# Four dot products on VectorE move from the lowest priority to the taps' priority

## The chip, the cores and the metric

The kernel runs on one core of a Trainium2 chip. The metric is the device time of one execution in microseconds (us); the time before is the median of three runs, 2440.19 us (2438.97 to 2441.34). The engines are called as in the profile: PE is TensorE (matmuls), PEld its weight loads, DVE is VectorE, ACT is ScalarE, POOL is GpSimd, SP is SyncE, which here only issues DMAs.

## The reference

A block of two layers works on 1024 latent tokens of width 1024. Layer 0 has a recurrent mixer, layer 1 a convolution mixer, and each layer ends with a gated feed-forward part with a 3x3 convolution over a grid of 16 rows by 64 columns. The mixers and feed-forward parts are scaled by six modulation vectors per layer, which are products of `silu(c)` with a 1024x6144 matrix:

```python
mod = s_c @ ada_w[i] + ada_b[i]
sh1, sc1, g1, sh2, sc2, g2 = [t[:, None, :] for t in jnp.split(mod, 6, axis=-1)]
...
xm2 = rmsnorm(h, norm_ffn[i]) * (1.0 + sc2) + sh2
h = h + g2 * conv_ffn(xm2, ffn_w_up[i], ffn_conv_w[i], ffn_conv_b[i], ffn_w_down[i], ROWS, GRID_W)
...
def conv_ffn(xm, w_up, cw, cb, w_down, rows, width):
    u = dwconv2d(xm @ w_up, cw, cb, rows, width)
    v, g = jnp.split(u, 2, axis=-1)
    return (jax.nn.silu(g) * v) @ w_down
```

`g2` of layer 0 is the second gate of that layer. It is needed when the first output of the first feed-forward part is added to `h`, and not before.

## The kernel before

Channels lie on the 128 partitions, tokens along the free axis. Every float32 product is made of three matmuls with a high and a low part of each operand (`xmh`, `xml` for data, `whi`, `wlo` for weights): a weight block is loaded into `wraw`, ACT copies it to `whi`, POOL or DVE subtracts to get `wlo` (`split`).

**The first feed-forward part** (`ffn` with l = 0, from line 1063 on) goes through 22 pairs p. A pair is two column tiles of the up-projection, each 128 channels by 1024 tokens, 48 matmuls, into one of three PSUM tiles in rotation (`nt % 3`). In this text the column tiles are numbered from 0: tiles 0 and 1 are pair 0, tiles 2 and 3 pair 1, and so on. After a column tile `ffn_conv` runs the nine taps of the convolution from PSUM into an SBUF tile `cv`: the centre tap on ACT (`cv<-ps,vec`), the other eight on DVE (`cv<-ps,vec,cv`). So a column tile cannot begin on PE before the taps of the tile three before it are done. Then ACT makes the silu (`cv<-cv`), DVE the product (`cv<-cv,cv`), ACT and POOL the parts `zh` and `zl`.

**The down-projection** runs between the up-projection's matmuls from pair 3 on (column tile 6): `between()` puts a `unit` of 12 matmuls after each four steps of a column tile. A unit writes the fourth PSUM tile, and DVE adds the unit's result times `g2` to `h` (`h<-ps,mod,h`, the flush). There is one such PSUM tile, so a unit waits on PE for the flush of the unit before. Its weights come in quarters (`load_down`): a load of 256 KB into `raw`, split into `dnh` and `dnl`.

**The gate.** `g2` of layer 0 has eight columns (numbers 40 to 47 of `mod`). Each is the product of a loaded 128x1024 block with `sC`, summed along the free axis (`ada_dot`, line 543). Columns 40 to 43 are made on DVE by one instruction each (`raw,mod<-raw,sC`), called in `first_tiles` of pair 0 (line 1157). Columns 44 to 47 are made by POOL (product) and ACT (sum), called in pairs 1 and 2 (line 1151); then `ada_bias` (line 1153) adds the bias on DVE (`mod<-mod,vec`). All flushes read the result.

**Two `raw` buffers** in rotation serve these blocks and the quarters of the down weights: columns 40, 42, 44, the quarter 0, column 47 and quarter 2 take the one (`raw_76`), columns 41, 43, 45, 46 and quarter 1 the other (`raw_77`). A buffer is loaded again when its last reader is done.

**What sets the order.** `Order` collects the instructions of DVE, ACT, POOL and SP in a pool while PE's matmuls are written in program order, with a duration for each from a formula. It always emits the instruction that can start first; among those that could start at the same time the smaller `prio` goes first, then the older (`_best`, lines 110 to 126). On the chip each engine runs its list in that order and waits in it. The taps of column tiles have priority 0, flushes -1, and the four dots on DVE priority 3. In `ada_dot` a `prio` that isn't zero also lets the load go without the wait for `after`.

Of the kernel before, what the change touches and what calls it, by code (L numbers as in the profile page):

```python
# [280 lines left out]
class Net:  # L281
# [258 lines left out]

    def ada_dot(self, l, q, eng="dve", after=(), prio=0):

        t, b = self.load_raw(self.a["ada"][l, q], after=() if prio else after)
        col, mB = self.mod[l][:, q:q + 1], self.modB[l][q // 8]
        if eng == "dve":
            self.stt(1024, t, t, 1.0, self.sC, MULT, MULT, [b, self.sCB], [b], [mB], accum=col, after=after, prio=prio)
        else:
            self.tten(1024, t, t, self.sC, MULT, [b, self.sCB], [b], eng=eng, prio=prio)  # L550
            self.act(1024, t, t, AF.Copy, [b], [b], [mB], accum=col)
# [511 lines left out]
    def ffn(self, l, end, last=None):  # L1063
# [40 lines left out]
        def quarter(g, q):  # L1104
            quarters[g, q] = load_down(g, q * 256, 256, dn.next())
# [12 lines left out]
        def zsplit(p, a, aB):  # L1118
            zh, zl, zhB, zlB = zr.next()
            Z[p] = zh, zl, [[zhB, zlB]] * 2  # L1120
            self.act(1024, zh, a, AF.Copy, [aB], [zhB])
            self.tten(1024, zl, a, zh.bitcast(F32), SUB, [aB, zhB], [zlB], eng="pool")

        def last_gate(f, pt, a, aB, acc, accB):

            zh, zl, zhB, zlB = zr.next()
            Z[NF - 1] = zh, zl, [[Buf(after=[b]) for b in (zhB, zlB)] for _ in range(2)]
            for h in range(2):
                b, c = Buf(after=[aB, accB]), slice(h * 512, h * 512 + 512)
                (hB, lB), av, gv = Z[NF - 1][2][h], a[:, c], acc[:, c]  # L1130
                self.ffn_conv(l, f, pt, acc, b, h * 8, h * 8 + 8, -2)
                silu = self.act(512, gv, gv, AF.Silu, [b], [b])
                self.tten(512, av, av, gv, MULT, [b], [b], prio=-3)
                self.act(512, zh[:, c], av, AF.Copy, [b], [hB])
                self.tten(512, zl[:, c], av, zh[:, c].bitcast(F32), SUB, [b, hB], [lB], prio=-3)
            self.sqrt_soon([silu])

        nt = 0
        ada = [(0, q) for q in range(40, 48)] + [(1, q) for q in range(48)] if l == 0 else []
# [4 lines left out]
        for p in range(NF):  # L1144
            if p >= 3 and p % 2 == 1 and p < NF - 1:
                g = (p - 3) // 2
                todo += [(g, q, d) for q in range(4) for d in (2 * q, 2 * q + 1)]
            pts, accs = [], []
            if ada and 0 < p < 3:
                for _ in range(2):  # L1150
                    self.ada_dot(*ada.pop(0), "pool", prio=3)
                if p == 2:
                    self.ada_bias(0, 5)
            for q in ((), (0,), (1, 2))[p] if p < 3 else ():
                quarter(0, q)
            if p == 0:
                self.first_tiles((0, 1), lambda ops: [self.ada_dot(*ada.pop(0), prio=3, after=ops) for _ in range(4)] if ada else None)
                pts, nt = [0, 1], 2
            for i, f in enumerate((p, NF + p)):
                if p:  # L1160
                    self.col_tile(self.w_next(), nt % 3, between)
                    pts.append(nt % 3)
                    nt += 1
                acc, accB = cv.next()
                accs.append((acc, accB))
                if f < 2 * NF - 1:
                    self.ffn_conv(l, f, pts[i], acc, accB)
            (a, aB), (gt, gB) = accs
            if p < NF - 1:
                self.act(1024, gt, gt, AF.Silu, [gB], [gB])  # L1170
                self.tten(1024, a, a, gt, MULT, [aB, gB], [aB])
                zsplit(p, a, aB)
            else:
                last_gate(2 * NF - 1, pts[1], a, aB, gt, gB)
            for _ in range(3 if p > 2 else 0):
                if ada:
                    self.ada_dot(*ada.pop(0), "pool", prio=3)
# [279 lines left out]
```

## Time and profile before

| | |
|---|---|
| median of three runs | 2440.19 us |
| the profiled execution: time | 2438.16 us |
| the profiled execution: span, first to last instruction | 2436.4 us |
| granted TensorE clock, mean over the span | 0.979 |
| first feed-forward part | about 560 to 1313 us of the span |

Of the profile four kinds of views are used: the page of the whole span, the waits (who waited for whom), the chain of work that ended last, and the timeline of an engine. A timeline row gives the start, the length, the engine, the line, the operation with output and input and the shape; rows that follow one another with the same names are merged (`x17` is 17 instructions). The brackets at its end give the idle time before the row and what ended it. A granted clock of 1.00 is 2.4 GHz, 0.50 is 1.2 GHz.

### The profile page before, as it was taken

What the parts mean: (1) busy time and instruction counts of PE and PEld (TensorE: products, weight loads), DVE (VectorE), ACT (ScalarE), POOL (GpSimd) and SP (SyncE); (2) the same over time, 40 slices, a digit from 0 to 9 for tenths busy, and PEclk for the clock granted to TensorE, in tenths of its full rate; (3) what the DMA queues carried; (4) which work ended last, traced back from release to release, by engine and by line L of the source; (5) the groups of instructions that cost most, each with busy time, mean ns of one, the idle gap of its engine ahead of it and who ended that gap; (6) DMA issues with size and microseconds to landing.
All of it is one profiled execution on the core that took longest, in us unless ns stands there. A gap on an engine that the chain in (4) does not pass through costs nothing.

```text
span 2436.4 us, 26124 instructions
## 1 busy us (share of the span) xinstructions
PE 2326.2 (95%) x10440; PEld 1892.8 (78%) x10440; DVE 1896.6 (78%) x1752; ACT 967.3 (40%) x1141; POOL 798.1 (33%) x409
## 2 busy tenths in 40 slices
PE   7999999889789999999999999889999999999997
PEld 2788888667578888888887888667888888888886
DVE  6677877776867777777878898677997777777878
ACT  4577777544233333333324333365322221222223
POOL 1100000354345544554523233245333322332323
PEclk9999999899899999999999999899999999999999
DMA  6324325253132323223211233422111111111101
GB/s 262 120 84 144 94 84 162 96 198 117 55 101 95 104 87 104 95 88 103 91 35 36 66 114 105 138 70 91 52 58 52 44 39 52 52 52 48 44 26 70
DMA packets 82442, 214.98 MB, mean 88 GB/s; under 512 B 8528, under 2 KB 33104, under 8 KB 82192
## 3 DMA queue, kind: packets, MB, share of 16 engines
q1 hardware_dynamic: 80448, 210.68, 26.3%
q10 hardware_dynamic: 1872, 2.62, 0.3%
q8 instruction: 82, 1.34, 0.2%
q14 instruction: 40, 0.33, 0.0%
HBM read 192.10 MB, written 13.63 MB: 84 GB/s over the span
## 4 chain that ended last, share of the span: by engine, by line
PE 70%; DVE 16%; ACT 5%; issue 3%; DMA 2%; POOL 2%; SPq 0%; ACTq 0%; DVEq 0%; POOLq 0%
PE ps L441 70%; DVE cv L362 4%; DVE CV L362 3%; DVE F L770 1%; ACT F L354 1%; POOL wlo L369 1%; DVE F L362 1%; DVE tt L362 1%; DVE F L369 1%; DVE rs L384 1%; ACT tt L354 1%; DVE raw L362 1%; ACT L354 1%; DVE h L362 1%; ACT whi L354 1%
## 5 line engine op out<-in xcount | busy, mean ns | idle before, releaser
L362 DVE SCALAR_TENSOR_TENSOR cv<-ps,vec,cv 128x960 f32<-128x960 f32 (+2 forms) x720 | 861.5, 1198 | 203.6 <-ACT cv L354 185.2
L441 PE MATMUL ps<-xmh,whi 128*128 128x512 f32 x2272 | 744.5, 394 | 19.7 <-ACT xmh L354 8.9
L441 PE MATMUL ps<-xmh,wlo 128*128 128x512 f32 x2272 | 738.0, 392 | 9.5 <-POOL wlo L369 5.9
L441 PE MATMUL ps<-xml,whi 128*128 128x512 f32 x2272 | 740.5, 393 | 4.6 <-DVE xml L362 4.2
L369 POOL TENSOR_TENSOR wlo<-wraw,whi 128x1024 fp32r<-128x1024 f32 (+1 forms) x164 | 399.8, 2442 | 712.6 <-ACT whi L354 694.9
L441 PEld LDWEIGHTS ps<-xmh,whi 128*128 128x128 f32 x2272 | 427.8, 189 | 115.9 <-ACT xmh L354 12.0
L441 PEld LDWEIGHTS ps<-xmh,wlo 128*128 128x128 f32 x2272 | 429.4, 189 | 103.1 <-POOL wlo L369 7.9
L441 PEld LDWEIGHTS ps<-xml,whi 128*128 128x128 f32 x2272 | 429.8, 189 | 102.4 <-DVE xml L362 9.4
L362 DVE SCALAR_TENSOR_TENSOR h<-ps,mod,h 128x1024 f32<-128x1024 f32 (+2 forms) x216 | 231.5, 1080 | 61.0 <-PE ps L441 60.8
L354 ACT ACTIVATE whi<-wraw 128x1024 fp32r<-128x1024 f32 (+1 forms) x198 | 205.2, 1042 | 123.3 <-PE ps L441 51.5
L354 ACT ACTIVATE cv<-ps,vec 128x1024 f32<-128x1024 f32 (+1 forms) x90 | 105.9, 1181 | 299.5 <-PE ps L441 280.5
L369 POOL TENSOR_TENSOR zl<-cv,zh 128x1024 fp32r<-128x1024 f32 x42 | 101.2, 2411 | 350.6 <-ACT zh L354 350.6
L441 PE MATMUL ps<-zh,dnh 128*128 128x512 f32 x576 | 180.1, 393 | 23.0 <-DVE h L362 23.0
L369 POOL TENSOR_TENSOR raw<-raw,sC 128x1024 f32<-128x1024 f32 x52 | 125.1, 2406 | 178.7 <-DMA raw<-ada_in 174.0
L441 PE MATMUL ps<-zl,dnh 128*128 128x512 f32 x576 | 181.4, 397 | 0.0
L441 PE MATMUL ps<-zh,dnl 128*128 128x512 f32 x576 | 177.8, 390 | 0.0
L354 ACT ACTIVATE raw<-raw 128x1024 f32<-128x1024 f32 x52 | 55.2, 1062 | 289.4 <-POOL raw L369 289.4
L354 ACT ACTIVATE cv<-cv 128x1024 f32<-128x1024 f32 (+1 forms) x46 | 47.0, 1022 | 293.5 <-DVE cv L362 293.3
L369 POOL TENSOR_TENSOR dnl<-raw,dnh 128x512 fp32r<-128x512 f32 x72 | 94.0, 1307 | 202.5 <-ACT dnh L354 202.5
L362 DVE SCALAR_TENSOR_TENSOR CV<-ps,vec,CV 128x1009 f32<-128x1009 f32 (+14 forms) x120 | 153.1, 1275 | 8.6 <-ACT CV L354 4.9
L441 PEld LDWEIGHTS ps<-zh,dnh 128*128 128x128 f32 x576 | 108.6, 189 | 45.9 <-DVE h L362 23.4
L441 PEld LDWEIGHTS ps<-zh,dnl 128*128 128x128 f32 x576 | 108.4, 188 | 26.4
(141 smaller groups left out, 2414.6 us busy)
## 6 DMA issues: line engine op xcount, KB each, us to landing
raw<-ada_in SPq DMA_DIRECT2D x88, 512.0 KB, 4.2
wraw<-up_in SPq DMA_DIRECT2D x88, 512.0 KB, 3.3
raw<-down_in SPq DMA_DIRECT2D x72, 256.0 KB, 3.2
wraw<-w_in SPq DMA_DIRECT2D x32, 512.0 KB, 3.3
wraw<-w_in_in SPq DMA_DIRECT2D x20, 512.0 KB, 3.9
wraw<-w_out_in SPq DMA_DIRECT2D x20, 512.0 KB, 3.7
wraw<-cw_in SPq DMA_DIRECT2D x16, 512.0 KB, 3.6
wraw<-gw_in SPq DMA_DIRECT2D x10, 512.0 KB, 3.4
```

Source lines behind the costliest of these rows:

```text
L354: "act", 0.21 + n * 0.00083, lambda: self.nc.scalar.activation(out, in_, func, **kw),
L362: lambda: self.nc.vector.scalar_tensor_tensor(out=out, in0=in0, scalar=scalar, in1=in1, op0=op0, op1=op1, **kw),
L369: return self.o.op(eng, dur, lambda: e.tensor_tensor(out=out, in0=in0, in1=in1, op=op), r, w, wp, prio=prio)
L384: return self.o.op("dve", 0.07 + n * 0.0063, lambda: self.nc.vector.reciprocal(out=out, in_=in_), r, w)
L441: self.nc.tensor.matmul(out, w, x, start=start, stop=stop)
L770: lambda t=t, a=a, ig=ig, rev=rev: nc.vector.tensor_tensor_scan(rev(t), rev(a), rev(ig), 0.0, op0=MULT, op1=ADD),
```

## The change

The four dots on DVE get priority 0, the taps' own, instead of 3. Since `prio` also switched off the wait of the load, a new argument `early` now does that, and the loads go as before. The dots on POOL keep priority 3; they had no `after`.

```diff
-    def ada_dot(self, l, q, eng="dve", after=(), prio=0):
+    def ada_dot(self, l, q, eng="dve", after=(), prio=0, early=False):
-        t, b = self.load_raw(self.a["ada"][l, q], after=() if prio else after)
+        t, b = self.load_raw(self.a["ada"][l, q], after=() if early else after)
...
-                self.first_tiles((0, 1), lambda ops: [self.ada_dot(*ada.pop(0), prio=3, after=ops) for _ in range(4)] if ada else None)
+                self.first_tiles((0, 1), lambda ops: [self.ada_dot(*ada.pop(0), early=True, after=ops) for _ in range(4)] if ada else None)
```

At one place on DVE, the taps of column tile 0, the list of before has these rows: two of the dots, then the taps of tile 0 (`cv_3479` from `ps_65`, eight instructions) and of tile 1.

```order
L362 SCALAR_TENSOR_TENSOR raw_77,mod_92<-raw_77,sC 128x1024
L362 SCALAR_TENSOR_TENSOR raw_76,mod_92<-raw_76,sC 128x1024
L362 SCALAR_TENSOR_TENSOR cv_3479<-ps_65,vec,cv_3479 128x960 x2
L362 SCALAR_TENSOR_TENSOR cv_3479<-ps_65,vec,cv_3479 128x16x63 x2
L362 SCALAR_TENSOR_TENSOR cv_3479<-ps_65,vec,cv_3479 128x15x63 x4
L362 SCALAR_TENSOR_TENSOR cv_3480<-ps_66,vec,cv_3480 128x960 x2
```

The list of the changed kernel at the same place:

```order
L362 SCALAR_TENSOR_TENSOR raw_77,mod_92<-raw_77,sC 128x1024
L362 SCALAR_TENSOR_TENSOR raw_76,mod_92<-raw_76,sC 128x1024
L362 SCALAR_TENSOR_TENSOR cv_3479<-ps_65,vec,cv_3479 128x960 x2
L362 SCALAR_TENSOR_TENSOR raw_77,mod_92<-raw_77,sC 128x1024
L362 SCALAR_TENSOR_TENSOR cv_3479<-ps_65,vec,cv_3479 128x16x63 x2
L362 SCALAR_TENSOR_TENSOR cv_3479<-ps_65,vec,cv_3479 128x15x63 x4
L362 SCALAR_TENSOR_TENSOR cv_3480<-ps_66,vec,cv_3480 128x960 x2
```

The fourth dot (column 43, on `raw_77`) now stands behind the second tap of column tile 0. In the list of before it stood behind the last tap of column tile 5, 46 taps later. The other three stand where they stood.

On ACT, between the silu of pair 0 (`cv_3480<-cv_3480`) and the centre tap of column tile 3 (`cv_3479<-ps_65,vec`), the list of before has the following. `raw_76,mod_92` and `raw_77,mod_92` are sums of gate columns, `dnh_3467` is quarter 1, `dnh_3469` quarter 2.

```order
L354 ACTIVATE cv_3480<-cv_3480 128x1024
L354 ACTIVATE raw_76,mod_92<-raw_76 128x1024
L354 ACTIVATE whi_80<-wraw_78 128x1024
L354 ACTIVATE zh_3471<-cv_3479 128x1024
L354 ACTIVATE dnh_3469<-raw_76 128x512
L354 ACTIVATE cv_3479<-ps_65,vec 128x1024
```

The changed kernel has there:

```order
L354 ACTIVATE cv_3480<-cv_3480 128x1024
L354 ACTIVATE raw_77,mod_92<-raw_77 128x1024
L354 ACTIVATE raw_76,mod_92<-raw_76 128x1024
L354 ACTIVATE zh_3471<-cv_3479 128x1024
L354 ACTIVATE whi_80<-wraw_78 128x1024
L354 ACTIVATE dnh_3467<-raw_77 128x512
L354 ACTIVATE dnh_3469<-raw_76 128x512
L354 ACTIVATE cv_3479<-ps_65,vec 128x1024
```

Two instructions have come in: the sum of column 46 and the split of quarter 1, which stood behind column tile 5 before. The bias of the gate (`mod_92<-mod_92,vec`) and the first flush moved on DVE likewise: the bias from behind the dot to behind the second tap of column tile 2, the first flush from behind the bias to before the last tap of column tile 4. The list of PE is the same in both.

## Rows read from the trace of the kernel before

**Rows 1.** The page: busy time, share of the span and instructions of two engines, and the shares of the chain that ended last.

```profile
PE 2326.2 (95%) x10440; PEld 1892.8 (78%) x10440; DVE 1896.6 (78%) x1752; ACT 967.3 (40%) x1141; POOL 798.1 (33%) x409
...
PE 70%; DVE 16%; ACT 5%; issue 3%; DMA 2%; POOL 2%; SPq 0%; ACTq 0%; DVEq 0%; POOLq 0%
```

**Rows 2.** The waits from 595 to 690 us: who waited for whom, us in total, times, the longest.

```profile
PE ps L441 <- DVE h L362: 23.0, 1, 23.0
...
DVE mod L369 <- ACT raw L354: 13.8, 1, 13.8
```

**Rows 3.** DVE's timeline around the fourth dot (658.30), the bias (674.54) and the first flush (674.82).

```profile
658.30 1.22 DVE L362 SCALAR_TENSOR_TENSOR raw<-raw,sC 128x1024 f32<-128x1024 f32 x1
...
674.54 0.17 DVE L369 TENSOR_TENSOR mod<-mod,vec 128x8 f32<-128x8 f32 x1 [13.75 <-ACT raw L354]
674.82 1.28 DVE L362 SCALAR_TENSOR_TENSOR h<-ps,mod,h 128x1024 f32<-128x1024 f32 x1
```

**Rows 4.** The same stretch on SP (two loads of gate columns issued from 659.55 on), POOL and ACT (the last of the gate's products and sums).

```profile
659.55 8.58 SPq L343 DMA_DIRECT2D raw<-ada_in  x2
...
670.99 2.34 POOL L369 TENSOR_TENSOR raw<-raw,sC 128x1024 f32<-128x1024 f32 x1 [4.40 <-DMA raw<-ada_in]
...
673.36 1.06 ACT L354 ACTIVATE raw<-raw 128x1024 f32<-128x1024 f32 x1 [5.59 <-POOL raw L369]
```

**Rows 5.** PE's timeline: the first unit (644.78) and the matmul behind it (647.54), the last matmuls before the second unit (652.54), the second unit (676.15) and the matmul behind it (680.83).

```profile
644.78 0.62 PE L441 MATMUL ps<-zh,dnh 128*128 128x512 f32 x2
...
647.54 0.62 PE L441 MATMUL ps<-xmh,whi 128*128 128x512 f32 x2
...
652.54 0.61 PE L441 MATMUL ps<-xmh,wlo 128*128 128x512 f32 x2
...
676.15 1.22 PE L441 MATMUL ps<-zh,dnh 128*128 128x512 f32 x2 [23.00 <-DVE h L362]
...
680.83 0.62 PE L441 MATMUL ps<-xmh,whi 128*128 128x512 f32 x2
```

**Rows 6.** Busy time by stretch (us, PE busy, PEld, DVE, ACT, POOL, granted clock, DMA share, GB/s) of the rest of the feed-forward part; and from the chain the piece that begins at 676.15.

```profile
681.00:1312.00 631.00, 631.00 (x2765) 518.94 (x2765) 492.64 (x432) 202.49 (x259) 294.86 (x140) 1.00 0.26 87
...
676.15 636.78 PE ps L441 x2780
```

**Rows 7.** DVE's timeline: the third dot and the first taps.

```profile
595.26 1.23 DVE L362 SCALAR_TENSOR_TENSOR raw<-raw,sC 128x1024 f32<-128x1024 f32 x1 [0.80 <-DMA raw<-ada_in]
...
596.41 21.08 DVE L362 SCALAR_TENSOR_TENSOR cv<-ps,vec,cv 128x960 f32<-128x960 f32 x17
```

**Rows 8.** PE's timeline: the first matmuls of column tile 3 and of column tile 5.

```profile
606.58 0.70 PE L441 MATMUL ps<-xmh,whi 128*128 128x512 f32 x2 [0.21 <-DVE cv L362]
...
628.46 0.62 PE L441 MATMUL ps<-xmh,whi 128*128 128x512 f32 x2
```

**Rows 9.** POOL's timeline: the weight split beside the first taps, and two earlier ones.

```profile
598.18 2.40 POOL L369 TENSOR_TENSOR wlo<-wraw,whi 128x1024 fp32r<-128x1024 f32 x1 [7.89 <-ACT whi L354]
...
518.16 2.50 POOL L369 TENSOR_TENSOR wlo<-wraw,whi 128x1024 fp32r<-128x1024 f32 x1 [3.61 <-ACT whi L354]
526.35 2.78 POOL L369 TENSOR_TENSOR wlo<-wraw,whi 128x1024 fp32r<-128x1024 f32 x1 [5.68 <-ACT whi L354]
```

**Rows 10.** DVE's timeline: an instruction with two inputs in SBUF, three times.

```profile
516.35 0.68 DVE L369 TENSOR_TENSOR xml<-raw,xmh 128x512 fp32r<-128x512 f32 x1
...
518.63 2.58 DVE L369 TENSOR_TENSOR xml<-raw,xmh 128x512 fp32r<-128x512 f32 x1 [0.21 <-ACT xmh L354]
...
526.79 2.89 DVE L369 TENSOR_TENSOR xml<-raw,xmh 128x512 fp32r<-128x512 f32 x1
```

**Rows 11.** The chain that ended last: taps on DVE (start, us). The third tap of tile 0, the last of tile 2 with the first of tile 3, the last of tile 4 with the first of tile 5.

```profile
598.91 1.28 DVE cv L362
...
626.21 2.34 DVE cv L362 x2
...
647.25 2.34 DVE cv L362 x2
```

**Rows 12.** Two idle times of PE, each with the first matmul after it, and the granted clock that followed (stretches as in rows 6).

```profile
515.82 0.50 PE L441 MATMUL ps<-xmh,whi 128*128 128x512 f32 x1 [2.30 <-DVE h L362]
...
516.00:520.00 4.00, 4.00 (x11) 3.12 (x12) 3.68 (x5) 2.58 (x4) 1.84 (x1) 0.57 0.45 176
520.00:522.00 2.00, 2.00 (x8) 1.32 (x7) 1.21 (x1) 0.00 (x0) 0.66 (x1) 1.00 0.14 35
...
1612.26 1.12 PE L441 MATMUL ps<-nacc,ones 128*128 128x512 f32 x2 [1.88 <-POOL nacc L369]
...
1612.00:1614.00 2.00, 1.74 (x6) 1.13 (x7) 0.69 (x1) 1.97 (x3) 0.20 (x1) 1.00 0.00 0
```

**Rows 13.** ACT's timeline: the silu of pair 0 and a sum of a gate column; the page's row on the loads of quarters (KB each, us to landing), and the landing times of the gate's blocks.

```profile
616.40 1.06 ACT L354 ACTIVATE cv<-cv 128x1024 f32<-128x1024 f32 x1 [6.38 <-DVE cv L362]
617.37 1.04 ACT L354 ACTIVATE raw<-raw 128x1024 f32<-128x1024 f32 x1
618.32 0.19 ACT L354 ACTIVATION_READ_ACCUMULATOR raw<-raw 128x1 f32 x1
...
raw<-down_in SPq DMA_DIRECT2D x72, 256.0 KB, 3.2
...
DMA to landing us min/median/max: 3.1/4.3/10.7
```

## The prediction

> **What bounds the kernel now.** I read four views in this order. The page says that PE is busy for 95% of the span and carries 70% of the chain that ended last [rows 1]; so only a stretch in which PE stands still, or is pushed back, can change the time. The waits from 595 to 690 us show one such stretch: PE waits 23.0 us, once, for a flush on DVE, and DVE waits 13.8 us for a sum on ACT [rows 2]. The timelines show why. The fourth dot runs at 658.30, behind all taps of column tiles 0 to 5 [rows 3]. Its buffer `raw_77` is free only then: SP issues the next gate blocks from 659.55 on, POOL multiplies the last of them at 670.99 after waiting 4.40 us for its load, ACT sums it from 673.36 [rows 4]. Then come the bias at 674.54 and the first flush at 674.82 [rows 3], and PE goes on with the second unit at 676.15 [rows 5]. From there the chain is 636.78 us of PE without another engine, and PE is busy 631.00 of 631.00 us from 681 to 1312 at a granted clock of 1.00 [rows 6]. What PE gains before 676 is kept to the end of this part, and since everything behind it starts from PE's end, to the end of the kernel.
>
> **The change part by part.**
>
> *The wait that goes.* In the changed order the fourth dot stands behind the second tap of tile 0, and the bias and the flush of the first unit come as early as PE wants them. Without the wait the second unit would begin one pair of matmuls after 652.54. The first unit has 12 matmuls between 644.78 and 647.54, 2.76 us, or 0.46 a pair, so at 653.00; it began at 676.15, 23.15 us later. It was also slow: from 676.15 to 680.83 is 4.68 us for the same 12 matmuls [rows 5], 1.92 more than 2.76, at the lower level of the clock that the long idle time had left. Together 25.07 us are to be had.
>
> *What is late next there.* The first flush now stands before the last tap of tile 4, whose end lies in the pair of taps that begins at 647.25 [rows 11]. With the delays of below (2.67 on DVE and 2.67 + 1.72 on PE) DVE reaches the flush at about 647.2 + 2.67 + 0.17 = 650.1, and the first unit ends on PE at 647.54 + 4.39 = 651.9. The flush takes 1.28 [rows 3] and ends near 653.3, and the second unit would begin at 653.00 + 4.39 = 657.4. It has 4 us to spare, so I cost it at nothing. What waits behind the flush on DVE is one tap of tile 4, and PE needs that tile's PSUM only for tile 7, after the second unit.
>
> *What the dot costs at its new place.* DVE is what PE waits for at that moment: column tile 3 begins at 606.58 after 0.21 us of waiting for the taps of tile 0 [rows 8]. So each microsecond that the dot takes there comes on top of PE's path. A dot moves the next instruction by 596.41 - 595.26 = 1.15 us [rows 7]. That is the lower bound. It starts where the third tap now starts, at 598.91 [rows 11], and POOL has then been at a weight split since 598.18, until 600.58 [rows 9]. The dot reads two SBUF tiles, `raw` and `sC`. No row of before has a dot beside a POOL instruction; the nearest with two SBUF inputs is the subtraction for `xml`. It takes 0.68 alone, but 2.58 and 2.89 when it starts after a POOL split [rows 10], and ends 0.55 after POOL both times: 518.63 + 2.58 = 521.21 against 518.16 + 2.50 = 520.66, and 529.68 against 529.13 [rows 9, 10]. So it waits for POOL's end and then needs its own length less 0.13. The dot would end at 600.58 + 1.23 - 0.13 = 601.68, and as its successor starts 595.26 + 1.23 - 596.41 = 0.08 before its end [rows 7], the third tap starts at 601.60 or, with 1.21 for the dot, 601.58: 2.67 later than 598.91. I take 2.67, as the row resembles the dot in both inputs.
>
> The taps beside the same split are not held: the third lasts 1.28 [rows 11], the mean of the seventeen is 21.08 / 17 = 1.24 [rows 7]. They read PSUM and one SBUF tile. The Trainium skill (SBUF — State Buffer, "Who interferes with whom") says that a VectorE instruction with two SBUF inputs contends with a GpSimd instruction that reads SBUF, that the one issued first has the port for its whole length, and that one SBUF input is free of this. This speaks against the change, as it puts a two-input instruction on the busiest stretch of VectorE; the rows on `xml` and on the taps agree. By the rule the dot costs 2.67, without it 1.15, and the rest of the sum is the same.
>
> *The clock.* PE's wait before tile 3 grows from 0.21 to 0.21 + 2.67 = 2.88 us. An idle time of 2.30 us at 515.82 was followed by a mean granted clock of 0.57 for 4 us, and 1.00 after; one of 1.88 us at 1612.26 by 1.00 [rows 12]. Mine is longer than the first, so I count it in: 4.00 x (1 - 0.57) = 1.72 us. The bounds are 0 and the 1.92 of the second unit above.
>
> *The rest.* The bias, 0.17 us [rows 3], now lies among the taps of tile 2. These end about 1.15 after 626.21 [rows 11], and tile 5, which needs them, begins at 628.46 [rows 8]: some 1.1 us of cover, and PE's own lateness by the clock adds to it. If that cover were gone it costs 0.17. The load of the dot's block went out before the taps in both kernels and isn't moved. Two products on POOL and two sums on ACT move from behind tile 5 to among tiles 0 to 2; POOL's busy share over the span is 33% [rows 1] and `w_next` has its weight splits made two column tiles ahead, 2 x 48 matmuls of 0.23 us or 22 us, so 5 us of products more are covered. On SP the loads of columns 45 and 46 and of quarter 1 come earlier and wait there for the dot and for ACT; what is queued behind them is quarter 0, quarter 2 and up-weights, which are loaded ahead of their splits; quarters 0 to 2 are first read in pair 3.
>
> *The sum.* 25.07 - 2.67 - 1.72 = 20.68 us. The profiled execution took 2438.16 us for a span of 2436.4, so it should become 2417.5 with a span of 2415.7. It lies 2.03 below the median of 2440.19, so the median becomes 2419.5.
>
> **The rivals.**
>
> *The dot is not held, or the clock does not fall.* For it: no row shows a dot beside POOL, and the clock followed idle times of this length only in a few rows. If the dot is held but the clock stays, the saving is 22.40 and the time 2417.8. If the dot isn't held, PE's wait is only 0.21 + 1.15 = 1.36, shorter than the 1.88 that left the clock alone, the saving is 25.07 - 1.15 = 23.92 and the time 2416.3.
>
> *Part of the wait comes back as another.* ACT's list now has the splits of quarters 1 and 2 before the centre tap of tile 3, and ACT waits in order for both loads. The silu of pair 0 starts at 616.40 + 2.67 = 619.1, two sums of 0.97 to 1.2 follow [rows 13], so quarter 2 goes out near 622.2, lands 3.2 later [rows 13], and the centre tap ends near 627.2. DVE wants it when tile 2's taps end, at 627.4 + 2.67 = 630.0. So 2.8 us are to spare, and from there each microsecond is on the path. The longest landing of a gate block is 10.7 [rows 13]; a quarter as late as that is 7.5 late and costs 4.7: 2424.2.
>
> *Slower than before.* The same place decides it, if the quarters' loads stand behind so much on SP that they land later than 3.2 + 2.8 + 20.7 = 26.7 us after issue. At 30 us the loss is 24.0 against 20.7 gained: 2443.5. Against it stands that no landing in the rows comes near that [rows 13].
>
> *The change takes away a wait that another would have held anyway.* Then PE would stop at the second unit for something else until about 676, and the time stays at 2440. Against it: the unit's own weights and data were used by the first unit already, and it began 0.05 after the flush's end (674.82 + 1.28) [rows 3, 5].
>
> **How the numbers follow.** Chances: the forecast 0.55, dot held with the clock up 0.15, dot not held 0.12, a late centre tap or a like wait 0.12, no change 0.03, slower 0.03. A difference of about 0.2%, 4.9 us, is what a measurement of this kernel can tell from no change. The first four cases are all faster by more than that: 0.94. Same 0.03, slower 0.03. The range goes from 2415.0, a little under the time without hold (the runs of before lie up to 1.2 off their median), to 2424.5, which takes in the late quarter.
>
> **What would show it right or wrong.** On DVE a dot behind two taps of tile 0, about 2.7 us long, ending 1.1 after a POOL split; on PE a wait of some 2.9 us for DVE's taps before tile 3 and a granted clock of 0.50 for some microseconds behind it; the bias near 622 and the first flush near 652, with the wait of 23.0 gone and the unit at 2.76 us. A dot of 1.2 us there would refute the hold, a clock of 1.00 the fourth term. The prediction as a whole is wrong if PE waits more than a few microseconds anywhere between 606 and 690, or if what is gained by 690 is not kept to the end.

## The result and the profile after

The changed kernel takes 2421.07 us (median of 4 runs, 2419.67 to 2422.58), the kernel before on the same chip 2439.58 (four runs, among them the three of the table above): a ratio of 0.9925 with a 95% interval of 0.9908 to 0.9942, 18.5 us faster. The forecast was 2419.5 us. The execution that was profiled took 2421.64 us for a span of 2419.9; by its own steps the forecast for the profiled one was 2417.5 and 2415.7.

The page of the changed kernel, busy time and the shares of the chain that ended last, beside [rows 1]:

```profile
PE 2328.7 (96%) x10440; PEld 1893.6 (78%) x10440; DVE 1897.9 (78%) x1752; ACT 966.6 (40%) x1141; POOL 798.6 (33%) x409
...
PE 74%; DVE 13%; ACT 4%; issue 2%; DMA 2%; POOL 1%; SPq 0%; ACTq 0%; DVEq 0%; POOLq 0%
```

The instructions are as many as before. What moved is the chain: PE's share rose from 70% to 74%, DVE's fell from 16% to 13%. The waits from 595 to 690 us, beside [rows 2]:

```profile
DVE h L362 <- PE ps L441: 4.4, 3, 3.3
...
PE ps L441 <- ACT dnh L354: 2.9, 1, 2.9
```

The 23.0 us wait of PE for the flush is gone, and so is DVE's 13.8 for the last gate sum. The flushes now wait for PE, not PE for them. What is left is one wait of 2.9 us. Its releaser reads ACT `dnh`; that is the last event before it, not its cause, as DVE shows (the dot at 597.09, the bias at 620.72, the first flush at 651.50; beside [rows 3, 7]):

```profile
594.70 2.47 DVE L362 SCALAR_TENSOR_TENSOR cv<-ps,vec,cv 128x960 f32<-128x960 f32 x2
597.09 2.87 DVE L362 SCALAR_TENSOR_TENSOR raw<-raw,sC 128x1024 f32<-128x1024 f32 x1
599.88 0.08 DVE L362 DVE_READ_ACCUMULATOR raw<-raw,sC 128x1 f32 x1
599.88 18.57 DVE L362 SCALAR_TENSOR_TENSOR cv<-ps,vec,cv 128x1008 f32<-128x1008 f32 x15
...
620.72 0.15 DVE L369 TENSOR_TENSOR mod<-mod,vec 128x8 f32<-128x8 f32 x1
...
651.50 1.28 DVE L362 SCALAR_TENSOR_TENSOR h<-ps,mod,h 128x1024 f32<-128x1024 f32 x1 [3.34 <-PE ps L441]
```

From 599.88 six taps of tile 0 are left, 18.57 / 15 = 1.24 us each, so they end at about 607.3; PE begins tile 3 at 607.54. In the fourth profile of the same kernel (see the repeats below) the same wait, 2.87 us, bears DVE `cv` as its releaser. The dot lies beside POOL's split (POOL's timeline):

```profile
596.47 2.40 POOL L369 TENSOR_TENSOR wlo<-wraw,whi 128x1024 fp32r<-128x1024 f32 x1 [7.89 <-ACT whi L354]
599.38 2.83 POOL L369 TENSOR_TENSOR raw<-raw,sC 128x1024 f32<-128x1024 f32 x1 [0.52 <-DMA raw<-ada_in]
603.42 2.38 POOL L369 TENSOR_TENSOR raw<-raw,sC 128x1024 f32<-128x1024 f32 x1 [1.21 <-DVE cv L362]
```

The split ends at 598.87 and the dot at 599.96, 1.09 later. PE's timeline, beside [rows 5, 8], with the wait before tile 3 (607.54), the first unit (648.54), the second (656.75) and the matmul behind it:

```profile
607.54 1.19 PE L441 MATMUL ps<-xmh,whi 128*128 128x512 f32 x2 [2.87 <-ACT dnh L354]
608.53 1.06 PE L441 MATMUL ps<-xml,whi 128*128 128x512 f32 x2
...
613.59 0.63 PE L441 MATMUL ps<-xml,whi 128*128 128x512 f32 x2
...
648.54 0.62 PE L441 MATMUL ps<-zh,dnh 128*128 128x512 f32 x2
...
656.75 0.62 PE L441 MATMUL ps<-zh,dnh 128*128 128x512 f32 x2
...
659.51 0.62 PE L441 MATMUL ps<-xmh,whi 128*128 128x512 f32 x2
```

The second unit takes 2.76 us and waits for nothing. Behind the wait of 2.87 the pairs of tile 3 start 0.85 apart instead of 0.45. The granted clock says why (stretches of PE alone: us, PE busy, granted clock, DMA share, GB/s):

```profile
608.00:610.00 2.00, 2.00 (x6) 0.50 0.84 285
...
614.00:616.00 2.00, 2.00 (x10) 1.00 0.00 0
653.00:676.00 23.00, 23.00 (x103) 1.00 0.07 24
676.00:1290.00 614.00, 614.00 (x2691) 1.00 0.26 87
```

For some 6 us PE was at 1.2 GHz. From there on it doesn't stop until the part ends. ACT, where the late centre tap of tile 3 was feared (pair 0's silu, the second wait for a quarter, the centre tap):

```profile
617.36 1.06 ACT L354 ACTIVATE cv<-cv 128x1024 f32<-128x1024 f32 x1 [8.55 <-DVE cv L362]
...
623.74 0.64 ACT L354 ACTIVATE dnh<-raw 128x512 fp32r<-128x512 f32 x1 [0.82 <-DMA raw<-down_in]
624.28 1.19 ACT L354 ACTIVATE cv<-ps,vec 128x1024 f32<-128x1024 f32 x1
```

ACT waits 0.82 us for the quarter and the centre tap is done at 625.5; PE waits nowhere for it.

**Where the time went.** Three rows of the chain of waits (start, us, matmuls) cut the span into parts: the last matmuls before the feed-forward part, the long piece that ends it, and the start of the second feed-forward part.

```profile
514.10 60.77 PE ps L441 x256
...
607.54 684.08 PE ps L441 x2984
...
1733.42 652.80 PE ps L441 x2882
```

Part A is from 514.10 + 60.77 = 574.87 to 607.54 + 684.08 = 1291.62, that is 716.75 us; part B from there to 1733.42, 441.80. The same marks of the kernel before, beside the piece of [rows 6], which ends at 676.15 + 636.78 = 1312.93:

```profile
515.82 60.77 PE ps L441 x256
...
1749.93 652.78 PE ps L441 x2882
```

They give A = 1312.93 - 576.59 = 736.34 and B = 437.00. So the feed-forward part saved 19.6 us, 1.7 were gained ahead of it (574.87 against 576.59), and 4.8 were lost again behind it, in layer 1's convolution mixer (`conformer` in the kernel, the conformer part below), where the order of the instructions on PE, DVE, ACT and POOL is the same in both. The experiments had to settle two things: whether the terms at tile 3 are what the forecast took them for, and whose the 4.8 us are.

### The profile page after: what moved, and what is told of

Its sections match the earlier page's. It is cut to its first block, busy times and chain, and to the rows that moved or that the text cites. A ratio compares the mean times of both kernels' runs of the same rounds, so it can differ in the third digit from the quotient of the medians.

```text
span 2419.9 us, 26120 instructions
## 1 busy us (share of the span) xinstructions
PE 2328.7 (96%) x10440; PEld 1893.6 (78%) x10440; DVE 1897.9 (78%) x1752; ACT 966.6 (40%) x1141; POOL 798.6 (33%) x409
## 4 chain that ended last, share of the span: by engine, by line
PE 74%; DVE 13%; ACT 4%; issue 2%; DMA 2%; POOL 1%; SPq 0%; ACTq 0%; DVEq 0%; POOLq 0%
PE ps L441 74%; DVE CV L362 2%; DVE F L770 1%; ACT F L354 1%; DVE cv L362 1%; DVE F L362 1%; DVE tt L362 1%; DVE F L369 1%; DVE rs L384 1%; POOL wlo L369 1%; ACT L354 1%; ACT tt L354 1%; DVE xml L362 1%; DVE raw L362 1%; DVE xml L369 1%
## 5 line engine op out<-in xcount | busy, mean ns | idle before, releaser
L441 PEld LDWEIGHTS ps<-zl,dnh 128*128 128x128 f32 x576 | 107.9, 187 | 24.6
```

The lines of the kernel that those rows point to most:

```text
L441: self.nc.tensor.matmul(out, w, x, start=start, stop=stop)
```

## The experiments

Theory: the stall was a chain on one shared buffer with the late dot at its head, and the dot's price at its new place is the time that POOL's split holds it. Rivals: the dot is long because of its place; its lateness alone made the stall; VectorE's time is paid wherever the dot stands; the conformer part is longer because of the change.

Measured in all of them (A and B by the rows as above; the same three marks in each profile, where A is in several pieces by the end of the last):

| profile | A | B | median of the runs, ratio to before |
|---|---|---|---|
| before, four profiles | 736.34, 736.28, 736.33, 736.18 | 437.00, 437.71, 441.10, 439.82 | |
| after, four profiles | 716.75, 713.94, 713.91, 713.95 | 441.80, 441.55, 440.81, 443.85 | 2421.07, 0.9925 |
| split behind the dot | 712.35 | 439.63 | 2417.38, 0.9906 (0.9891 to 0.9921) |
| dot behind tile 1 | 712.63 | 439.73 | 2415.58, 0.9897 (0.9880 to 0.9913) |
| dot on POOL | 711.53 | 437.93 | 2416.21, 0.9900 (0.9885 to 0.9915) |
| own buffer, old priority | 711.68 | 443.10 | 2416.86, 0.9901 (0.9886 to 0.9916) |
| own buffer, late dot | 722.26 | 443.00 | 2427.52, 0.9948 (0.9932 to 0.9965) |

A repeats within 0.2 us, except in the one profile in which the clock fell. So differences of a few tenths of a microsecond can be read there, which the times can't show.

### POOL's split behind the dot

```diff
-self.stt(1024, t, t, 1.0, self.sC, MULT, MULT, [b, self.sCB], [b], [mB], accum=col, after=after, prio=prio)
+op = self.stt(1024, t, t, 1.0, self.sC, MULT, MULT, [b, self.sCB], [b], [mB], accum=col, after=after, prio=prio)
+if (l, q) == (0, 43):
+    cB = Buf()
+    cB.w = [op]
+    self.hold = self.wq_use + 2, self.tten(1, self.modc[:, :1], col, col, MULT, [cB], [], eng="pool")
...
```

In the part that is left out here, the weight split of column tile 4 takes that instruction as one more input to wait for.

> From the changed kernel: the fourth dot stays behind the second tap of tile 0, and POOL's weight split of column tile 4 now waits for it (a one-element POOL instruction that reads the dot's column stands ahead of the split). Theory (the dot took 2.87 us because the split, 596.47 to 598.87, holds the port that both want): the dot is about 1.2 us long, ending some 1.1 to 1.2 us after its start; PE waits about 1.2 to 1.5 us before tile 3 instead of 2.87, its clock either stays (then the pairs of tile 3 start 0.45 us apart, and the kernel is 4.2 to 4.5 us faster than the changed one) or still falls (then 1.5 us faster). The split itself ends about 1.5 us later, which column tile 4 has to spare. Rival (the dot is long because of its place between the taps, with whatever POOL does): the dot stays near 2.9 us, PE's wait near 2.87 us, and the time that of the changed kernel within 0.5 us.

DVE's dot, POOL's small instruction with the split behind it, and PE's start of tile 3:

```profile
598.88 1.22 DVE L362 SCALAR_TENSOR_TENSOR raw<-raw,sC 128x1024 f32<-128x1024 f32 x1
```

```profile
600.18 0.19 POOL L369 TENSOR_TENSOR modc<-mod 128x1 f32<-128x1 f32 x1 [9.78 <-DVE raw L362]
600.33 2.40 POOL L369 TENSOR_TENSOR wlo<-wraw,whi 128x1024 fp32r<-128x1024 f32 x1
```

```profile
607.69 0.70 PE L445 MATMUL ps<-xmh,whi 128*128 128x512 f32 x2 [1.20 <-DVE cv L362]
608.22 0.63 PE L445 MATMUL ps<-xml,whi 128*128 128x512 f32 x2
```

At the same place between the taps the dot takes 1.22 us, PE waits 1.20 and its clock stays up. A is 1.56 to 1.60 us below the three profiles of the changed kernel in which its clock stayed too (see the repeats below), and 4.4 below the first, where it fell; 2.67 - 1.15 = 1.52 is the part of the forecast's term that was put down to the hold. The hold is shown, and the place is not what makes the dot long.

### The dot behind the taps of tile 1

```diff
-self.first_tiles((0, 1), lambda ops: [self.ada_dot(*ada.pop(0), early=True, after=ops) for _ in range(4)] if ada else None)
+self.first_tiles((0, 1), lambda ops: [self.ada_dot(*ada.pop(0), early=True, after=ops) for _ in range(3)] if ada else None)
...
+if p == 0 and ada:
+    self.ada_dot(*ada.pop(0), early=True, after=[self.tap])
```

`self.tap` is the last tap written so far, here that of tile 1.

> From the changed kernel: the fourth dot stands behind the taps of tile 1 instead of behind the second tap of tile 0; its load and its early block stay as in the changed kernel. Theory (all of what the dot costs is that tile 0's taps are what PE waits for; behind tile 1's taps VectorE has about 1.1 us to spare against PE): PE's wait before tile 3 is back at about 0.2 us with the clock at 1.00, the first flush still finds the bias done, and PE does not wait for the second unit; 4 to 5.5 us faster than the changed kernel, some 2416. If POOL's product holds the dot there too, up to 1.6 us of that comes back as a wait before tile 4. Rival (the dot's time has to be paid wherever it stands, since VectorE is what PE follows through the whole first part): a PE wait of 1.2 to 2.9 us appears at another tile, and the time is within 1.5 us of the changed kernel. A second rival (a late bias: the dot now ends too late and the flush waits): PE idles again at the second unit by more than 3 us, slower than the changed kernel.

```profile
615.16 1.22 DVE L362 SCALAR_TENSOR_TENSOR raw<-raw,sC 128x1024 f32<-128x1024 f32 x1
```

```profile
605.45 0.70 PE L441 MATMUL ps<-xmh,whi 128*128 128x512 f32 x2 [0.56 <-DVE cv L362]
```

Here the dot is free of POOL and is not paid at tile 3: the wait of 0.56 is 0.35 above that of the kernel before, and the taps also start 0.40 later after the mark of part A (595.28 - 575.06 = 20.22, before 596.41 - 576.59 = 19.82), as the third dot's block landed later (DVE waits 1.20 us for it, before 0.80). A is 1.3 us below the changed kernel's usual one (713.9), not the 2.67 of the dot. From the start of tile 3 to the end of A it takes 1287.69 - 605.45 = 682.24 us, the run with its own buffer below 1286.35 - 605.07 = 681.28: some 1 us is paid behind tile 3. Against that run half of it is there when the first unit begins (644.12 - 605.45 = 38.67, there 643.27 - 605.07 = 38.20): PE waited for DVE's taps before tile 5, at 627.68. The other half comes within that unit, which ends 41.89 behind the start of tile 3 and there 40.96: PE waits for POOL's `zl` at 646.31, and the chain that leads there goes back over loads of gate blocks and quarters into `raw`. The time, 2415.6, is what the theory said. The first rival falls: no wait of 1.2 us or more appears at another tile, and the time is 5.5 us below the changed kernel. It has a point only in the half microsecond before tile 5. The second falls too, as PE does not wait at the second unit.

### The dot on POOL and ACT

```diff
-[self.ada_dot(*ada.pop(0), early=True, after=ops) for _ in range(4)]
+[self.ada_dot(*ada.pop(0), "dve" if i < 3 else "pool", early=True, after=ops) for i in range(4)]
```

> From the changed kernel: the fourth dot goes to POOL (the product) and ACT (the sum) instead of VectorE, with its load as early. Theory (the block's buffer is what counted; VectorE's 2.87 us are what is paid for it): no dot between tile 0's taps, PE's wait before tile 3 about 0.2 us at clock 1.00, ACT and POOL have the time; 4 to 5.5 us faster than the changed kernel, some 2416. Rival (POOL's and ACT's work for the dot delays the splits that the column tiles wait for, or POOL's products hold VectorE's taps): a PE wait of over 1 us appears in the first ten tiles, and the time is within 2 us of the changed kernel, on either side.

```profile
605.80 0.70 PE L441 MATMUL ps<-xmh,whi 128*128 128x512 f32 x2 [0.20 <-ACT raw L354]
```

The wait before tile 3 is back at 0.20, the clock stays, and A is 736.28 - 711.53 = 24.75 below the kernel before (736.28 is the mean of its four). This is the forecast's 25.07 with nothing to be taken off, 0.3 short.

### A buffer of its own for the fourth block

From the kernel before, with the priority as it was:

```diff
+own = None
+if (l, q) == (0, 43):
+    own = Ring([self.cv[2]])
-t, b = self.load_raw(self.a["ada"][l, q], after=() if prio else after)
+t, b = self.load_raw(self.a["ada"][l, q], own, after=() if prio else after)
```

> From the kernel before, with the dots at their old low priority: the fourth block alone is loaded into a buffer of its own (one that is free until the third tap chain), so that the buffer that the later blocks 44 to 47 take is not held by it. The planner then sets the fourth dot early, ahead of tile 0's taps. Theory (the 23 us stall was a chain on one shared buffer: the late dot held it, so the loads of later blocks and their POOL and ACT steps came late and the bias with them): the bias stands before the first flush is due, PE's idle at the second unit is under 1 us, and the time is 20 to 25 us below the kernel before, at or up to 4 us below the changed kernel. Rival (the priority itself is needed, the dot still comes late and the flush waits for it): PE's stall stays above 15 us and the time within 8 us of the kernel before.

DVE's fourth dot (592.46, now in `cv`), the third, and the bias:

```profile
592.46 1.22 DVE L362 SCALAR_TENSOR_TENSOR cv<-cv,sC 128x1024 f32<-128x1024 f32 x1
...
593.74 1.23 DVE L362 SCALAR_TENSOR_TENSOR raw<-raw,sC 128x1024 f32<-128x1024 f32 x1
...
618.26 0.16 DVE L369 TENSOR_TENSOR mod<-mod,vec 128x8 f32<-128x8 f32 x1
```

PE's start of tile 3, behind its only wait between 598 and 680 us:

```profile
605.07 0.70 PE L441 MATMUL ps<-xmh,whi 128*128 128x512 f32 x2 [0.60 <-DVE cv L362]
```

A is 24.60 below the kernel before with no change of priority: the dot now runs ahead of the third one, mostly in the time in which DVE waited 0.80 us for the third block [rows 7]; the taps start 594.89 - 574.67 = 20.22 us after the mark, 0.40 later than before. So the priority is one cure and not the only one. This run doesn't tell the buffer from the dot's lateness, as both went. The next one does.

### Own buffer, but the dot as late as before

From the kernel before:

```diff
+own = Ring([(self.ttall[:, :1024], Buf(after=[x for _, x in self.tt.items]))])
...
+if p == 2 and ada:
+    self.ada_dot(0, 43, prio=3, after=[self.tap])
+    self.ada_bias(0, 5)
...
```

Column 43 is also taken out of the list of the other blocks, and the bias out of its old place; `self.tap` is as above, here the last tap of tile 5.

> From the kernel before: the fourth block has a buffer of its own, but its dot is forced to stand behind the last tap of tile 5, as late as before (about 658 us), with the bias behind it. So the other blocks no longer wait for its buffer, while the dot is as late as it was. Theory (the stall is two parts in one chain: the dot's own lateness up to about 660, and the load, POOL's product and ACT's sum that followed on its buffer, 659.55 to 674.54): the first flush comes at about 661 to 663 instead of 674.82, PE's idle at the second unit falls from 23.0 to 8 to 11 us, and the time is 12 to 15 us below the kernel before, some 2425. Rival (the dot's own place among the taps is the whole cause): the flush and PE's idle stay as they were, the time within 3 us of the kernel before. Rival (the buffer is the whole cause): PE's idle under 2 us, and the time 20 us or more below the kernel before.

The dot, the bias and the first flush on DVE, and the second unit on PE:

```profile
658.99 1.22 DVE L362 SCALAR_TENSOR_TENSOR tt<-tt,sC 128x1024 f32<-128x1024 f32 x1
...
660.25 0.17 DVE L369 TENSOR_TENSOR mod<-mod,vec 128x8 f32<-128x8 f32 x1
660.52 1.28 DVE L362 SCALAR_TENSOR_TENSOR h<-ps,mod,h 128x1024 f32<-128x1024 f32 x1
```

```profile
661.86 1.22 PE L441 MATMUL ps<-zh,dnh 128*128 128x512 f32 x2 [8.02 <-DVE h L362]
```

The dot is as late as in [rows 3], but the bias follows it at once and PE waits 8.02 us instead of 23.00. A is 736.28 - 722.26 = 14.02 us shorter. So both parts of the stall are shown: 8 us are the dot's own lateness, 15 the load, the product and the sum that stood behind its buffer [rows 4]. Both rivals fall.

### The two kernels again, three times each

> The changed kernel once more, for a second profile. Question: 19.6 us were saved by the stat matmul at 1283 us, but only 16.5 at the end of the profiled executions, with the clock lower at other places behind 1400 us than in the kernel before. If this is chance of the clock from execution to execution, the stretches behind 1283 us differ by 1 to 4 us between two profiles of this same kernel, at places that change. If the change does it, the second profile shows the same stretches as the first within 0.5 us.

> The kernel before once more, for a second profile. If the losses behind 1283 us are chance, this profile's stretches from there to the end differ from the first one's by 1 to 4 us too, and the 1.7 us by which the changed kernel was ahead before it reached the third dot are within what two profiles of the same kernel differ by. If not, both agree within 0.5 us.

> The changed kernel a third time. Two profiles of it had the same 2.87 us wait before tile 3, but only in the first did the clock fall behind it (pairs 0.85 us apart for 6 us; in the second 0.45 from the start), and from the end of the statistics matmuls to the start of the second FFN's weights they took 425.4 and 425.2 us, against 420.6 and 421.3 in two profiles of the kernel before. Theory A (the clock's falls are chance of the execution): the fall at tile 3 comes in some profiles and not in others, worth 0 or 2.8 us, and the later stretch scatters so that the two kernels overlap. Theory B (the change makes the later stretch longer): its length is 424 us or more again.

> The kernel before a third time. Theory A (chance): the stretch behind the FFN comes out between 420 and 426 us, not always under 422. Theory B (the change makes it longer): under 422 us again. By both, PE's idle at the second unit stays 23.0 to 23.2 us.

> The changed kernel a fourth time, with the same two theories: by A the stretch behind the FFN overlaps that of the kernel before over four profiles each, by B it is 424 us or more.

> The kernel before a fourth time: by A the stretch behind the FFN lies between 420 and 426 us and overlaps that of the changed kernel, by B it is under 422 us.

PE's start of tile 3 in the second profile of the changed kernel:

```profile
609.84 0.70 PE L441 MATMUL ps<-xmh,whi 128*128 128x512 f32 x2 [2.87 <-ACT dnh L354]
610.37 0.63 PE L441 MATMUL ps<-xml,whi 128*128 128x512 f32 x2
610.84 0.62 PE L441 MATMUL ps<-xmh,wlo 128*128 128x512 f32 x2
```

The wait is the same, and the clock does not fall: three of four profiles have it so, and A is 2.82 us shorter in them than in the first. So the fall at tile 3 is chance of the execution. The row from which the forecast took its clock term is such a case too: ahead of the matmuls that lead up to part A, PE waits 2.30 or 2.31 us in all thirteen profiles, and these 256 matmuls then take about 60.8 us in seven of them (60.77 in the first profile of either kernel, shown above) and 59.2 in six, as in the second profile of the changed kernel:

```profile
517.99 59.19 PE ps L441 x256
```

The same is seen in the conformer part. In the first profile of the changed kernel and in the second one PE begins a piece behind the same wait of 1.70 us:

```profile
1664.18 0.50 PE L441 MATMUL ps<-xmh,wlo 128*128 128x512 f32 x1 [1.70 <-POOL wlo L369]
```

```profile
1664.00:1690.00 26.00, 24.86 (x98) 0.93 0.34 112
```

```profile
1665.06 0.50 PE L441 MATMUL ps<-xmh,wlo 128*128 128x512 f32 x1 [1.70 <-POOL wlo L369]
```

```profile
1665.00:1690.00 25.00, 23.98 (x101) 1.00 0.34 116
```

The stretches of PE around it (granted clock 0.93 and 1.00) and the chain, which gives that piece of 69 matmuls 17.98 us in the first and 16.35 in the second, show that the clock fell in one of them. Part B of one and the same kernel differs by up to 4.1 us between profiles (437.00 to 441.10 before, 440.81 to 443.85 after). (By the marks of the expectations, which begin 16.4 us behind part A's end, at the matmuls of the norm's statistics, B is 16.4 shorter: 424.7 and 423.4 for the kernel before, 424.4 and 427.5 for the changed one.) Of theory B the half on the kernel before, always under 422, falls; the half on the changed kernel, always 424 or more, stands. The two sets still overlap by only 0.3 us, and their means, 438.9 and 442.0, are 3.1 apart; the five other kernels, whose instructions there are in the same order, lie from 437.9 to 443.1.

What the 3.1 us consist of can be read in part. PE's busy time in B, for the same matmuls, is 407.36, 408.89, 411.48 and 409.57 us in the four profiles of before and 411.25, 410.82, 409.50 and 411.75 in the four of after, on average 1.5 more. PE takes longer for them at the lower clock (0.98 granted in the first of before, 0.97 in the others); in the kernel before the spread of 4.12 is the whole spread of B. The rest is waiting, and about 1.0 of it lies at one place. PE waits there 2.11 to 2.28 us in the four of before, 2.49 in the first of after and 3.35 to 3.49 in the other three. In those three DVE's `cxl`, an instruction with two SBUF inputs, begins 1.0 to 1.2 us before the end of a weight split on POOL and takes 2.04 to 2.27 us; in the other five it begins behind the split, or at most 0.34 before its end, and takes 1.23 to 1.42. Where it begins clearly before the split's end it ends 1.08 behind it, as the fourth dot did (1.09). The third profile of after (DVE, POOL, PE) and the first of before (DVE, POOL):

```profile
1519.21 2.04 DVE L369 TENSOR_TENSOR cxl<-raw,cxh 128x1024 fp32r<-128x1024 f32 x1 [0.75 <-ACT cxh L354]
...
1517.81 2.36 POOL L369 TENSOR_TENSOR wlo<-wraw,whi 128x1024 fp32r<-128x1024 f32 x1 [1.77 <-ACT whi L354]
...
1522.00 0.36 PE L441 MATMUL ps<-cxh,whi 128*128 128x256 f32 x1 [3.49 <-DVE yt L377]
```

```profile
1544.17 1.23 DVE L369 TENSOR_TENSOR cxl<-raw,cxh 128x1024 fp32r<-128x1024 f32 x1 [0.37 <-ACT cxh L354]
...
1541.60 2.41 POOL L369 TENSOR_TENSOR wlo<-wraw,whi 128x1024 fp32r<-128x1024 f32 x1 [0.45 <-ACT whi L354]
```

So the hold is met once more, at a place whose instructions the change left as they were. Whether the changed kernel is longer in B on average, for instance because it gets there at another time, or four profiles each fell so, is not settled; the two kernels with the old priority and a buffer of its own for the block have 443.1 and 443.0. The 1.7 us ahead of part A are chance: its start is at 574.3 to 576.9 in the four of before and at 574.0 to 577.2 in the four of after.

## Why the prediction was right, and where not

- *The wait that goes, 25.07.* Right. The run with the dot on POOL, which takes nothing off, saves 24.75.
- *What is late next there.* Right: the first flush waits 3.34 us for PE and ends at 651.50 + 1.28 = 652.78, and the second unit begins at 656.75, 4.0 later.
- *What the dot costs, 2.67.* Right in mechanism and size. PE's wait went from 0.21 to 2.87, forecast 2.88; the dot ends 1.09 after the split, forecast 1.10; behind the dot the split no longer holds it (1.22). Part A with the clock up says it once more: 736.28 - 713.93 = 22.35, forecast for this case 25.07 - 2.67 = 22.40. So the trace agrees with the rule of the Trainium skill that the forecast cited (SBUF — State Buffer, "Who interferes with whom").
- *The clock, 1.72.* This is the step that failed: "Mine is longer than the first, so I count it in". Length alone does not decide. The wait of 2.87 was followed by a fall in one profile of four, and there it cost 2.82, more than the 1.92 that was set as the upper bound; in three it cost nothing, which was the rival "dot held with the clock up". That bound was one unit of 12 matmuls at the low level; tile 3 goes on longer, and 14 of its matmuls ran from 607.54 to 613.59, 6.05 us. And the row that the term was worked out from, a fall behind 2.30 us of waiting at 515.82, is itself a matter of the execution: the same wait has no fall behind it in six of the thirteen profiles.
- *The rest at nothing.* Right: the bias at 620.72 makes nobody wait, POOL and ACT had the time.
- *Rivals.* The late centre tap did not come: the quarter kept ACT 0.82 us. Slower and no change did not come either, as there is no PE wait above 2.9 us between 606 and 690.
- *What is gained by 690 is kept to the end.* Only in part. Part A saved 22.35 in three profiles and 19.5 in one, 21.6 on average; part B was 3.1 longer on average, and 21.6 - 3.1 = 18.5 is also what the medians differ by, though most of their runs are other executions. The step "everything behind it starts from PE's end" left out that B itself varies, by the clock and by where a two-input instruction meets a POOL split. That the forecast of 20.68 came within 2.2 us of the 18.5 therefore rests in part on two misses of opposite sign: a clock term that is mostly nothing, and a longer part B, of which the forecast had no term.

## What to carry to other kernels

When an engine waits long for a small result, look for who holds the buffer of the work ahead of it: one late consumer here held back three later steps on three other engines, and 15 of the 23 us were theirs. Before a two-input VectorE instruction is put on the path, look at what GpSimd does at that moment: the same dot took 1.22 or 2.87 us. And compare kernels by the length of the part that was changed, in more than one profile: here it repeated within 0.2 us but for one fall of the clock, where whole executions of the kernel before lay between 2435.2 and 2444.5.

The dot on POOL, the dot behind tile 1 and the own buffer are each below the changed kernel in A by 1.3 to 2.4 us and in their medians by 4 to 5.5; these medians lie within 1.3 us of each other, so none of them is shown to be best. By A, with one profile each, the dot on POOL and the own buffer are level (711.53 and 711.68) and the dot behind tile 1 is 1 us longer.

## What was not expected of the hardware

- After the same idle time of PE the clock falls in one execution and stays in the next: 2.87 us (one fall in four profiles) and 1.70 us (17.98 and 16.35 us for the same 69 matmuls). What decides is not in these profiles.
- The hold goes both ways in one place: POOL's product behind the split began at 599.38, while the dot was still under way until 599.96, and took 2.83 us instead of the 2.38 of the next one.
